# The om products of a gated attention and mLSTM layer dealt out between groups of the neighbouring projections

## The chip, the cores and the metric

The kernel runs on one core of a Trainium2 chip. The metric is the device time of one execution in microseconds (us), as the median of several runs of the same program. Lower is better. A profile is one further execution, taken with the hardware profiler on; its span runs from the first to the last recorded instruction.

## The reference, cut to what matters

One layer is computed for 256 tokens of width 1024, all in float32: an attention branch with 8 heads and an mLSTM branch with 4 heads, each multiplied with gates, summed, and projected back.

```python
h = _rmsnorm(x, norm_w) * (1 + scale) + shift
(qa, ka, va, za, qm, km, vm, zm, om, ig, fg, ga, gm) = jnp.split(h @ w_in, SPLIT_IDX, axis=-1)
...
ya = (ya * jax.nn.silu(za)) @ w_att_proj
...
hm = jax.nn.sigmoid(heads(om, ML_HEADS).astype(f32)) * hm
hm = _rmsnorm(hm, ml_norm_w.reshape(ML_HEADS, 1, ML_HEAD_DIM))
ym = (merge(hm).astype(x.dtype) * jax.nn.silu(zm)) @ w_ml_proj

y = jax.nn.sigmoid(ga) * ya + jax.nn.sigmoid(gm) * ym
return x + gate * (y @ w_out)
```

Nearly all the work is `h @ w_in` (1024 x 11272) and three more products with 1024 x 1024 weights. In the text, "om" is the projection whose sigmoid multiplies the mLSTM output, "vm" the mLSTM's values, "ga" and "gm" the two final gates, "ml" the projection `w_ml_proj`, and "att" the result of `w_att_proj`.

## The kernel before

**Groups.** After a first phase (normalisation, modulation, and the q and k projections of the attention) the weights go by in 98 groups. A group is two 128-row slices of a weight matrix, mostly 512 columns wide. Each float32 weight is split into a high part `wh` (ACT, a cast, L481) and a rest `wl` (DVE, a subtraction, L485; for eight groups POOL does it), and TensorE (PE) multiplies high by high, low by high and high by low. The function `split(g)` does the two steps for group g. The buffers for `wh` and `wl` hold five groups (`HB = 5`), and the main loop at step g first splits group g + 4, then evacuates the PSUM tile that has just been finished, then runs the step's hooks (small pieces of other work, listed by `at`), and then issues the matmuls of group g. So ACT and DVE work up to four groups ahead of PE, and the cast of split g + 4 cannot start before PE has finished group g - 1.

**Order of the groups before.** va 0 to 11, za 12 to 19, qm 20 to 27, km 28 to 35, att 36 to 43, zm 44 to 51, vm 52 to 59 (its first half 52 to 55, its second 56 to 59), om 60 to 73, ga 74 to 81, gm 82 to 89, ml 90 to 97, and the output projection. Each half of a segment has four groups and one PSUM tile (two such tiles, "mm").

**om by sums.** om is not multiplied in the plain way. Its weight is cut into 2 x 2 blocks of 512 x 512, and seven block products replace eight, in the manner of Strassen. Sums of rows of h (`h_full`, `h_sum`: P5, P6, P3, P7) are made on DVE and ACT while vm runs. Four sums of weight blocks are made in DRAM: eight DMAs from the POOL queue (`om_sum`, L746 and L748, four of them adding onto DRAM), issued at steps 10, 15, ... 45. The seven products collect in four PSUM banks ("aux", 128 x 512): bank 0 by products 0 and 2, bank 1 by 1 and 3, bank 2 by 4 and 6, bank 3 by 5. Between two products of one bank, `ev_om` takes the bank over: after product 0 ACT copies it with its sign turned (omu, L790), after product 1 DVE adds (omu, L792), after 3 DVE adds (omv, L796), after 4, 5 and 6 DVE subtracts (L798, L801, L804) and ACT takes the sigmoid (L785). A product is two groups of 6 matmuls; a vm group is 12 matmuls of the same size, a ga or gm group is 24 matmuls of half the width.

**After om.** Two groups at a time, `ml_num` (L872 to L879) multiplies the scores with vm, DVE multiplies with om's sigmoid and ACT takes the squares; `ml_y` (L887 to L898) normalises two heads over DVE, POOL and DVE; `ml_T` (L909 to L914) transposes the result on PE for the ml product, ACT and DVE splitting it (`ymh`, `yml`). `ev_ga` (L811, L812) evacuates ga's tile with a sigmoid on ACT into a buffer of its own (slot s5, which the scores occupied until then) and multiplies with att on POOL.

**Loads.** Weights come through six buffers ("raw", 1 MB each) by DMAs from SP's queue, in the order of the list `loads`. A buffer is refilled when its last split is done; `issue` keeps to the list's order.

Of the kernel before, what the change touches and what calls it, by code (L numbers as in the profile page):

```python
# [9 lines left out]
F32 = mybir.dt.float32  # L10
F32R = mybir.dt.float32r
AF = mybir.ActivationFunctionType
OP = mybir.AluOpType
# [38 lines left out]
OM_FIRST = (0, 1, 4, 5)  # L52
OM_SUMS = ((0, (0, 0), False), (2, (0, 1), False), (0, (0, 1), True), (2, (1, 1), True),
           (1, 0, False), (1, (1, 1), True), (3, 1, False), (3, (1, 0), True))
OM_SUM_AT = 10
W_PIECES = ((0, 512), (512, NR), (512, 1024), (1024, NR))


# [13 lines left out]
def tile_hybrid(ctx: ExitStack, tc: tile.TileContext, x, c, params2, w_row, w_va, ada_mod, ada_gate,  # L72
# [274 lines left out]
    seg("ws", wml, 0, "ml", "ym")  # L347
    seg("tok", wout, 0, "out", "y")
    NCH = len(chunks)
    C, G0, place = {}, [], []  # L350
    for i, ch in enumerate(chunks):
        C[ch["name"], ch["half"]] = i
        G0.append(len(place))
        place += [(i, kp) for kp in range(2 if ch["kind"] == "sums" else 4)]
    NG = len(place)
    G0.append(NG)

    def start(name, half=0):
        return G0[C[name, half]]

    def done(name, half):
        return G0[C[name, half] + 1]

    loads = []
    raw_of = {}
    last_use = {}

    def add_load(fn):
        loads.append(fn)
        return len(loads) - 1  # L370
# [6 lines left out]
    def mk_single(i, q):  # L377
        def f():
            v = raw_tile()[:, 0:4 * NV]
            nc.sync.dma_start(v, w_va[i, q])  # L380
            return v.rearrange("p (k n) -> p k n", k=4)
        return f

    def mk_pair(src, c0, kp):
        def f():
            t = raw_tile()
            v = t.rearrange("p (k n) -> p k n", k=2)
            nc.sync.dma_start(v, src[:, 2 * kp:2 * kp + 2, c0:c0 + 1024])
            return v
        return f  # L390

    om_sums = [dram.tile([128, 4, 512], F32, name=f"om_sum{i}") for i in range(4)]

    def om_block(kh, nh):
# [6 lines left out]
    def mk_block(blk):  # L401
        def f():
            v = raw_tile().rearrange("p (k n) -> p k n", k=4)
            nc.sync.dma_start(v, om_operand(blk))
            return v
        return f
# [1 line left out]
    NSINGLE = 3  # L408
    GSEG = ("km", "att", "zm", "vm")
    gate_loads = []  # L410
    for i, ch in enumerate(chunks):
        if i < NSINGLE:
            for q in range(2):
                li = add_load(mk_single(i, q))
                for g in (2 * q, 2 * q + 1):
                    raw_of[4 * i + g] = (li, slice(2 * (g % 2), 2 * (g % 2) + 2), slice(0, ch["n"]))
                last_use[li] = 4 * i + 2 * q + 1
        elif ch["kind"] == "sums":
            li = add_load(mk_block(ch["blk"]))
            for kp in range(2):  # L420
                raw_of[G0[i] + kp] = (li, slice(2 * kp, 2 * kp + 2), slice(0, 512))
            last_use[li] = G0[i] + 1
        elif ch["half"] == 0:
            if ch["name"] in GSEG:
                gate_loads.append(add_load(mk_pair(ada_gate, 0, len(gate_loads))))
            for kp in range(4):
                li = add_load(mk_pair(ch["src"], ch["c0"], kp))
                for hf in range(2):
                    raw_of[G0[i + hf] + kp] = (li, slice(0, 2), slice(hf * 512, hf * 512 + 512))
                last_use[li] = G0[i + 1] + kp  # L430
    xload = add_load(lambda: None)

    issued = [0]
# [26 lines left out]
    def slot(tag, shape, dt, name):  # L460
        free(tag)
        return hl.tile(shape, dt, name=name, tag=tag, bufs=1)
# [317 lines left out]
    def ev_om(j):  # L780
        om, b = T["om"], T["ombank"]
        part = [[om[:, t, 512 * n:512 * n + 512] for n in range(2)] for t in range(2)]

        def put(t, n, src):
            nc.scalar.activation(part[t][n], src, AF.Sigmoid)  # L785

        if j == 0:
            T["u"] = hl.tile([128, 2, 512], F32, name="omu", tag="scr", bufs=2)
            T["v"] = hl.tile([128, 2, 512], F32, name="omv", tag="scr", bufs=2)[:, 0]
            nc.scalar.mul(T["u"][:, 0], b[0], -1.0)  # L790
        elif j == 1:
            nc.vector.tensor_tensor(T["u"][:, 1], b[1], T["u"][:, 0], op=OP.add)  # L792
        elif j == 2:
            put(0, 0, b[0])
        elif j == 3:
            nc.vector.tensor_tensor(T["v"], b[1], T["u"][:, 0], op=OP.add)  # L796
        elif j == 4:
            nc.vector.tensor_tensor(part[1][1], T["v"], b[2], op=OP.subtract)  # L798
            put(1, 1, part[1][1])
        elif j == 5:  # L800
            nc.vector.tensor_tensor(part[1][0], b[3], T["v"], op=OP.subtract)  # L801
            put(1, 0, part[1][0])
        else:
            nc.vector.tensor_tensor(part[0][1], T["u"][:, 1], b[2], op=OP.subtract)  # L804
            put(0, 1, part[0][1])

    def ev_ga(pt, half):
        if half == 0:
            T["ga"] = slot("s5", [128, KT, S], F32, "gat")
        v = T["ga"][:, 4 * half:4 * half + 4]  # L810
        nc.scalar.activation(v, pt, AF.Sigmoid)  # L811
        nc.gpsimd.tensor_tensor(v, v, T["att"][:, 4 * half:4 * half + 4], op=OP.mult)  # L812

    def ev_gm(pt, half):
        if half == 0:
# [115 lines left out]

    def gate_read():
        gd = T["gd"]
        T["gateb"] = slot("s4", [128, D], F32, "gateb")
        nc.sync.dma_start(T["gateb"], bass.AP(tensor=gd.tensor, offset=gd.offset, ap=[[0, 128], [1, D]]))

    def load_x():
# [78 lines left out]
    for q, name in enumerate(("P5", "P6", "P3", "P7")):  # L1016
        at(s + 1 + q, h_sum, name)
    for hp in range(2):
        s = done("om", 6) + 3 * hp
        at(s + 1, ml_num, 2 * hp)  # L1020
        at(s + 2, ml_num, 2 * hp + 1)
        at(s + 3, ml_y, hp)
        at(s + 7, ml_T, 2 * hp)
        at(s + 8, ml_T, 2 * hp + 1)
# [24 lines left out]
    for g in range(NG):  # L1049
        ci, kp = place[g]  # L1050
        ch = chunks[ci]
        if g + A < NG:
            split(g + A, hooks_between.get(g, []))
            consumed.update(li for li in cons.get(g + A, []) if li not in gate_loads)
        if kp == 0:
            if ci > 0:
                pc = chunks[ci - 1]
                if pc["kind"] == "sums":
                    ev_om(pc["half"])
                elif pc["name"] in EV and ci - 1 != C["za", 0]:  # L1060
                    EV[pc["name"]](mmt[ci - 1], pc["half"])
                elif pc["name"] == "out":
                    for t in range(2):
                        ev_out(mmt[ci - 1][:, t], pc["half"] * 512, 512, t)
            sh = [128, 2, 512] if ch["kind"] == "tok" else [128, 4, 256]
            if ch["kind"] == "sums":
                if ch["half"] == 0:
                    T["ombank"] = []
                if ch["bank"] == len(T["ombank"]):
                    T["ombank"].append(aux([128, 512]))  # L1070
            elif ci < NCH - 1:
                mmt[ci] = ps.tile(sh, F32, name="mm", bufs=2)
                if ch["kind"] == "tok":
                    mmt[ci] = mmt[ci][:, :, 0:ch["n"]]
# [113 lines left out]
```

## Time and profile before

| | us |
|---|---|
| median of 3 runs | 355.19 (354.45 to 355.51) |
| the profiled execution's own time | 355.22 |
| its span | 353.4 |
| PE busy in the span | 344.1 |
| DVE busy | 268.3 |
| ACT busy | 220.5 |
| granted PE clock | 1.00 in every slice |

The span and the time of the profiled execution differ by 1.8 us. PE's busy time counts each matmul from its start to its end, and matmuls overlap: consecutive 512-wide ones start 0.23 us apart and are recorded with 0.39 us each. So PE's idle time is less than what PE loses; the losses are seen in the distance from start to start.

### The profile page before, as it was taken

The page shows a single profiled execution, that of the slowest core. Times are in us where ns is not written, and L with a number is a line of the kernel's source. Part 1 is how long each engine was busy: PE and PEld are TensorE (multiplying, and loading weights), DVE is VectorE, ACT ScalarE, POOL GpSimd, SP SyncE. Part 2 cuts the span into 40 slices and gives each one's busy share as a digit, 9 for nine tenths or more (in the row PEclk, how much of TensorE's full clock was granted, in tenths as well). Part 3 has the DMA queues.
Part 4 walks back from the last instruction along what each step waited for, and adds up shares of the span by engine and source line. Part 5 has one row for each costly group of instructions (what it writes and reads, how often), then busy time and mean ns, then how long its engine had stood idle before and what let it go on. Part 6 is the DMA issues. An engine that isn't in the chain of part 4 may idle for free.

```text
span 353.4 us, 6216 instructions
## 1 busy us (share of the span) xinstructions
PE 344.1 (97%) x2420; PEld 320.2 (91%) x2420; DVE 268.3 (76%) x390; ACT 220.5 (62%) x344; POOL 101.3 (29%) x89
## 2 busy tenths in 40 slices
PE   7999999999999999999999999998999999999996
PEld 7787889999999999999998888876799989999996
DVE  6989987966984348978847778789755667799961
ACT  4858789799777857657437654498454336932510
POOL 4600003942304473457005542000002212093000
PEclk9999999999999999999999999999999999999999
DMA  8999999883783899796996987569749007781011
GB/s 303 417 414 415 415 418 410 218 357 123 267 327 121 189 308 238 270 417 153 310 426 197 273 337 258 198 227 365 239 87 366 26 2 231 305 280 79 2 59 61
DMA packets 27309, 89.33 MB, mean 253 GB/s; under 512 B 3176, under 2 KB 5104, under 8 KB 26096
## 3 DMA queue, kind: packets, MB, share of 16 engines
q1 hardware_dynamic: 24408, 80.02, 61.2%
q0 software_dynamic: 2720, 8.39, 10.5%
q10 hardware_dynamic: 152, 0.53, 0.5%
q8 instruction: 19, 0.31, 0.3%
q14 instruction: 10, 0.08, 0.1%
HBM read 87.68 MB, written 9.64 MB: 275 GB/s over the span
## 4 chain that ended last, share of the span: by engine, by line
PE 69%; DVE 13%; issue 10%; ACT 5%; POOL 3%; ACTq 0%; POOLq 0%; DVEq 0%
PE pm L203 13%; PE mm L1120 8%; PE mm L1118 8%; PE mm L1121 8%; DVE wl L485 7%; PE mm L1113 5%; PE mm L1111 5%; PE mm L1112 5%; ACT wh L481 3%; PE mm L1104 1%; DVE kmT L715 1%; DVE omt L898 1%; PE xps L268 1%; PE aux L675 1%; PE mm L1133 1%
## 5 line engine op out<-in xcount | busy, mean ns | idle before, releaser
L485 DVE TENSOR_TENSOR wl<-raw,wh 128x1024 fp32r<-128x1024 f32 (+1 forms) x98 | 128.3, 1333 | 46.6 <-ACT wh L481 46.4
L481 ACT CAST wh<-raw 128x1024 fp32r<-128x1024 f32 (+1 forms) x106 | 105.1, 1016 | 27.6 <-DMA raw<-in_w_in_dram 11.3
L1118 PE MATMUL mm<-hTh,wh 128*128 128x256 f32 x320 | 90.1, 281 | 0.0
L1120 PE MATMUL mm<-hTl,wh 128*128 128x256 f32 x320 | 88.7, 277 | 0.0
L1121 PE MATMUL mm<-hTh,wl 128*128 128x256 f32 x320 | 88.7, 277 | 0.0
L1120 PEld LDWEIGHTS mm<-hTl,wh 128*128 128x128 f32 x320 | 60.2, 188 | 0.0
L1118 PEld LDWEIGHTS mm<-hTh,wh 128*128 128x128 f32 x320 | 60.2, 188 | 0.0
L1121 PEld LDWEIGHTS mm<-hTh,wl 128*128 128x128 f32 x320 | 60.2, 188 | 0.0
L1111 PE MATMUL mm<-wh,hTh 128*128 128x512 f32 (+1 forms) x112 | 40.6, 362 | 0.0
L1112 PE MATMUL mm<-wl,hTh 128*128 128x512 f32 (+1 forms) x112 | 40.2, 359 | 0.0
L1113 PE MATMUL mm<-wh,hTl 128*128 128x512 f32 (+1 forms) x112 | 40.2, 359 | 0.0
L485 POOL TENSOR_TENSOR wl<-raw,wh 128x1024 fp32r<-128x1024 f32 x8 | 20.5, 2573 | 16.7 <-ACT wh L481 16.7
L1113 PEld LDWEIGHTS mm<-wh,hTl 128*128 128x128 f32 x112 | 21.0, 188 | 2.5
L188 ACT CAST wrh<-raw 128x512 fp32r<-128x512 f32 (+1 forms) x24 | 18.2, 761 | 8.1 <-DMA raw<-in_w_row_dram 8.1
L1111 PEld LDWEIGHTS mm<-wh,hTh 128*128 128x128 f32 x112 | 21.1, 188 | 2.4
L1112 PEld LDWEIGHTS mm<-wl,hTh 128*128 128x128 f32 x112 | 21.1, 188 | 2.4
L193 DVE TENSOR_TENSOR wrl<-raw,wrh 128x512 fp32r<-128x512 f32 (+1 forms) x26 | 20.5, 813 | 1.4 <-ACT wrh L188 1.4
L203 PE MATMUL pm<-wrh,hTh 128*128 128x512 f32 x64 | 20.0, 393 | 0.0
L203 PE MATMUL pm<-wrh,hTl 128*128 128x512 f32 x64 | 19.9, 392 | 0.0
L203 PE MATMUL pm<-wrl,hTh 128*128 128x512 f32 x64 | 19.2, 398 | 0.0
L891 POOL TENSOR_SCALAR f<-f 128x4 f32<-128x4 f32 x2 | 0.4, 198 | 62.9 <-DVE f L890 62.9
L1121 PE MATMUL mm<-ymh,wl 128*128 128x256 f32 x64 | 17.7, 276 | 0.0
(245 smaller groups left out, 755.1 us busy)
## 6 DMA issues: line engine op xcount, KB each, us to landing
raw<-in_w_in_dram SPq DMA_DIRECT2D x31, 1024.0 KB, 7.4
adat<-in_ada_mod_dram SPq DMA_DIRECT2D x16, 512.0 KB, 8.8
om_sum<-in_w_in_dram POOLq DMA_DIRECT2D x6, 1024.0 KB, 10.0
raw<-in_w_va_dram SPq DMA_DIRECT2D x6, 688.0 KB, 8.9
raw<-in_ada_gate_dram SPq DMA_DIRECT2D x4, 1024.0 KB, 7.5
raw<-in_w_att_proj_dram SPq DMA_DIRECT2D x4, 1024.0 KB, 9.0
raw<-om_sum SPq DMA_DIRECT2D x4, 1024.0 KB, 5.1
raw<-in_w_ml_proj_dram SPq DMA_DIRECT2D x4, 1024.0 KB, 5.3
```

The lines of the kernel that those rows point to most:

```text
L188: copy(wsp[k][0][:, c0:c1], wrow[k][:, c0:c1])
L193: e.tensor_tensor(l[:, cs], wrow[k][:, cs], h[:, cs].bitcast(F32), op=OP.subtract)
L203: nc.tensor.matmul(pm[ch][:, t], a[:, k, t * 128:(t + 1) * 128], b[:, cs], start=k == 0 and i == 0, stop=k == KT - 1 and i == 2)
L268: nc.tensor.matmul(o, v, diag[:, t], start=t == 0 and kk == 0, stop=t == 1 and kk == 1, skip_group_check=True)
L481: nc.scalar.copy(h, w)
L485: e.tensor_tensor(l, w, h.bitcast(F32), op=OP.subtract)
L1111: nc.tensor.matmul(o, a, wh[:, kk], start=first, stop=False)
L1112: nc.tensor.matmul(o, a, wl[:, kk], start=False, stop=False)
L1113: nc.tensor.matmul(o, b, wh[:, kk], start=False, stop=last)
L1118: nc.tensor.matmul(o, wh[:, kk, cs], sh_[:, k], start=first and i % 2 == 0, stop=False, skip_group_check=True)
L1120: nc.tensor.matmul(o, wh[:, kk, cs], sl_[:, k], start=False, stop=False, skip_group_check=True)
L1121: nc.tensor.matmul(o, wl[:, kk, cs], sh_[:, k], start=False, stop=last and i % 2 == 1, skip_group_check=True)
```

## The change

The seven om products no longer stand together. `place`, which lists the groups in PE's order, now deals them out: after the first group of vm's second half, seven times one further group (vm's other three, then the four of ga's first half) and then the two groups of one om product. om begins at group 58, and ga's second half at 78; gm begins at 82 and ml at 90 as before. Three things follow in the same diff.

- Loads are listed in the order of first use. ga's weights come as four loads of four slices by 512 columns instead of four loads of two slices by 1024 columns, so that the first half can come without the second.
- `ev_ga` puts the sigmoid into a small buffer and multiplies att in place on POOL, so that it no longer needs slot s5; the row of the output gate (`gateb`) takes slot s5 instead of att's slot s4.
- The DMAs that sum om's blocks are issued at steps 6, 11, ... 41 instead of 10, 15, ... 45. `ev_om` now stands before the step's split, not behind it, and the second pair of heads' hooks (`ml_num`, `ml_y`, `ml_T`) follow the first pair's by 2 steps instead of 3.

```diff
-OM_SUM_AT = 10
+OM_SUM_AT = 6
...
+    for i, ch in enumerate(chunks):
+        if ch["kind"] == "sums" or ch["name"] == "ga" and ch["half"] == 0:
+            continue
+        if (ch["name"], ch["half"]) != ("vm", 1):
+            place += [(i, kp) for kp in range(4)]
+            continue
+        whole = [(ci, kp) for ci in (i, C["ga", 0]) for kp in range(4)]
+        place += whole[:1]
+        for j in range(7):
+            place += whole[1 + j:2 + j] + [(C["om", j], kp) for kp in range(2)]
...
+    def mk_quad(src, c0, q):
+        def f():
+            v = raw_tile().rearrange("p (k n) -> p k n", k=4)
+            nc.sync.dma_start(v, src[:, 4 * q:4 * q + 4, c0:c0 + 512])
+            return v
+        return f
...
     def ev_ga(pt, half):
-        if half == 0:
-            T["ga"] = slot("s5", [128, KT, S], F32, "gat")
-        v = T["ga"][:, 4 * half:4 * half + 4]
-        nc.scalar.activation(v, pt, AF.Sigmoid)
-        nc.gpsimd.tensor_tensor(v, v, T["att"][:, 4 * half:4 * half + 4], op=OP.mult)
+        T["ga"] = T["att"]
+        v = T["att"][:, 4 * half:4 * half + 4]
+        w = hl.tile([128, 4, S], F32, name="gat", tag="scr", bufs=2)
+        nc.scalar.activation(w, pt, AF.Sigmoid)
+        nc.gpsimd.tensor_tensor(v, v, w, op=OP.mult)
...
-        T["gateb"] = slot("s4", [128, D], F32, "gateb")
+        T["gateb"] = slot("s5", [128, D], F32, "gateb")
...
     for hp in range(2):
-        s = done("om", 6) + 3 * hp
+        s = done("om", 6) + 2 * hp
...
     for g in range(NG):
         ci, kp = place[g]
         ch = chunks[ci]
+        pi = ended.get(g)
+        if pi is not None and chunks[pi]["kind"] == "sums":
+            ev_om(chunks[pi]["half"])
         if g + A < NG:
             split(g + A, hooks_between.get(g, []))
...
+        if pi is not None:
+            pc = chunks[pi]
+            if pc["name"] in EV and pi != C["za", 0]:
+                EV[pc["name"]](mmt[pi], pc["half"])
```

Where the order stood out by hand before, it is shown by what is queued on the engines. DVE's queue before, from the splits of om's product 2 (products count from 0) to the addition that follows product 3 (omv); L485 is a split's subtraction, raw_2381, raw_2416, raw_2438, raw_2459 and raw_2506 are the loads of products 2 to 6, L740 belongs to vm's evacuation, and aux is the PSUM bank that an addition reads:

```order
L485 TENSOR_TENSOR wl_2555<-raw_2381,wh_2554 128x1024
L740 TENSOR_TENSOR vml_2478<-mm_2482,vaug_2477 128x2x512
L485 TENSOR_TENSOR wl_2568<-raw_2381,wh_2567 128x1024
L485 TENSOR_TENSOR wl_2580<-raw_2416,wh_2579 128x1024
L485 TENSOR_TENSOR wl_2594<-raw_2416,wh_2593 128x1024
L485 TENSOR_TENSOR wl_2606<-raw_2438,wh_2605 128x1024
L792 TENSOR_TENSOR omu_2583<-aux_2586,omu_2583 128x512
L485 TENSOR_TENSOR wl_2617<-raw_2438,wh_2616 128x1024
L485 TENSOR_TENSOR wl_2629<-raw_2459,wh_2628 128x1024
L485 TENSOR_TENSOR wl_2640<-raw_2459,wh_2639 128x1024
L485 TENSOR_TENSOR wl_2652<-raw_2506,wh_2651 128x1024
L796 TENSOR_TENSOR omv_2584<-aux_2586,omu_2583 128x512
```

DVE's queue at the same place in the changed kernel; L504 is the split's subtraction, raw_2381 is product 2, raw_2483 product 3, raw_2531 product 4, raw_2416 and raw_2533 are the two loads of ga's first half:

```order
L504 TENSOR_TENSOR wl_2547<-raw_2381,wh_2546 128x1024
L504 TENSOR_TENSOR wl_2563<-raw_2381,wh_2562 128x1024
L504 TENSOR_TENSOR wl_2576<-raw_2416,wh_2575 128x1024
L811 TENSOR_TENSOR omu_2543<-aux_2566,omu_2543 128x512
L504 TENSOR_TENSOR wl_2587<-raw_2483,wh_2586 128x1024
L504 TENSOR_TENSOR wl_2603<-raw_2483,wh_2602 128x1024
L759 TENSOR_TENSOR vml_2474<-mm_2478,vaug_2473 128x2x512
L504 TENSOR_TENSOR wl_2615<-raw_2416,wh_2614 128x1024
L504 TENSOR_TENSOR wl_2630<-raw_2531,wh_2629 128x1024
L504 TENSOR_TENSOR wl_2661<-raw_2531,wh_2660 128x1024
L504 TENSOR_TENSOR wl_2673<-raw_2533,wh_2672 128x1024
L815 TENSOR_TENSOR omv_2544<-aux_2566,omu_2543 128x512
```

The addition to omu stood behind both splits of product 3 and the first of product 4; now it stands ahead of both splits of product 3, and a ga split stands between the products.

POOL's queue before, from the last sums of om's blocks to the low parts of the mLSTM's q and k (qms, kms); om_sum1 and om_sum3 are blocks in DRAM, and the rows with DMA issue transfers:

```order
L746 DMA om_sum1_566<-in_w_in_dram 512x1x512
L485 TENSOR_TENSOR wl_1923<-raw_1562,wh_1922 128x1024
L748 DMA om_sum3_568<-om_sum1_566 16x16384
L843 TENSOR_TENSOR kms_2187<-kmT_1790,kms_2187 128x512
L843 TENSOR_TENSOR qms_2188<-qmT_1513,qms_2188 128x1024
L746 DMA om_sum3_568<-in_w_in_dram 512x1x512
```

POOL's queue at this place in the changed kernel:

```order
L765 DMA om_sum1_566<-in_w_in_dram 512x1x512
L504 TENSOR_TENSOR wl_1787<-raw_1562,wh_1786 128x1024
L504 TENSOR_TENSOR wl_1895<-raw_1729,wh_1894 128x1024
L504 TENSOR_TENSOR wl_1923<-raw_1562,wh_1922 128x1024
L767 DMA om_sum3_568<-om_sum1_566 16x16384
L765 DMA om_sum3_568<-in_w_in_dram 512x1x512
L862 TENSOR_TENSOR kms_2188<-kmT_1791,kms_2188 128x512
L862 TENSOR_TENSOR qms_2189<-qmT_1514,qms_2189 128x1024
```

The addition into om_sum1 moved ahead of two more splits on POOL, and the last addition, into om_sum3, moved ahead of kms and qms.

More of the change, by code (lines that the diff above doesn't have):

```diff
@@ L349, in tile_hybrid @@
     NCH = len(chunks)
-    C, G0, place = {}, [], []
+    C = {}
     for i, ch in enumerate(chunks):
         C[ch["name"], ch["half"]] = i
-        G0.append(len(place))
-        place += [(i, kp) for kp in range(2 if ch["kind"] == "sums" else 4)]
-    NG = len(place)
-    G0.append(NG)
+    place = []
+    for i, ch in enumerate(chunks):
[8 more added lines that the diff above has]
+            place += whole[1 + j:2 + j] + [(C["om", j], kp) for kp in range(2)]
+    NG = len(place)
+    G0, GE_ = {}, {}
+    for g, (ci, kp) in enumerate(place):
+        G0.setdefault(ci, g)
+        GE_[ci] = g + 1
+    ended = {g: ci for ci, g in GE_.items()}
     def start(name, half=0):
@@ L361, in done @@
     def done(name, half):
-        return G0[C[name, half] + 1]
+        return GE_[C[name, half]]
     loads = []
     raw_of = {}
+    quad, pair = {}, {}
     last_use = {}
@@ L410, in tile_hybrid @@
     gate_loads = []
[L411 to L430, printed above, removed]
+    for g, (i, kp) in enumerate(place):
+        ch = chunks[i]
+        if kp == 0 and ch["name"] in GSEG and ch["half"] == 0:
+            gate_loads.append(add_load(mk_pair(ada_gate, 0, len(gate_loads))))
+        if ch["kind"] == "sums":
+            if kp == 0:
+                add_load(mk_block(ch["blk"]))
+            raw_of[g] = (len(loads) - 1, slice(2 * kp, 2 * kp + 2), slice(0, 512))
+        elif i < NSINGLE or ch["name"] == "ga":
+            if kp % 2 == 0:
+                quad[i] = add_load(mk_single(i, kp // 2) if i < NSINGLE else mk_quad(ch["src"], ch["c0"] + 512 * ch["half"], kp // 2))
+            raw_of[g] = (quad[i], slice(2 * (kp % 2), 2 * (kp % 2) + 2), slice(0, ch["n"]))
+        else:
+            if ch["half"] == 0:
+                pair[ch["name"], kp] = add_load(mk_pair(ch["src"], ch["c0"], kp))
+            c0 = 512 * ch["half"]
+            raw_of[g] = (pair[ch["name"], kp], slice(0, 2), slice(c0, c0 + 512))
+        last_use[raw_of[g][0]] = g
     xload = add_load(lambda: None)
@@ L1054, in tile_hybrid @@
             consumed.update(li for li in cons.get(g + A, []) if li not in gate_loads)
-        if kp == 0:
[L1056 to L1064, printed above, removed]
+        if pi is not None:
+            pc = chunks[pi]
+            if pc["name"] in EV and pi != C["za", 0]:
+                EV[pc["name"]](mmt[pi], pc["half"])
+            elif pc["name"] == "out":
+                for t in range(2):
+                    ev_out(mmt[pi][:, t], pc["half"] * 512, 512, t)
+        if kp == 0:
             sh = [128, 2, 512] if ch["kind"] == "tok" else [128, 4, 256]
```

## The prediction

> **What bounds the kernel now.** I read the page first, then PE's waits, then the stretch around om instruction by instruction.
>
> ```profile
> PE 344.1 (97%) x2420; PEld 320.2 (91%) x2420; DVE 268.3 (76%) x390; ACT 220.5 (62%) x344; POOL 101.3 (29%) x89
> ```
>
> PE is the bound almost everywhere, so time can only come from PE's own losses. The list of PE's waits (who waited, for whom, us in total, times, longest) says where these are; L1094 is the first matmul of an om group, L909 the transposes of ml_T, L855 the scores:
>
> ```profile
> PE aux L1094 <- DVE omu L792: 1.6, 1, 1.6
> PE aux L909 <- DVE omt L898: 0.7, 2, 0.4
> PE aux L1094 <- DVE omt L798: 0.5, 1, 0.5
> PE aux L1094 <- ACT omu L790: 0.4, 1, 0.4
> PE aux L855 <- POOL qms L843: 0.3, 1, 0.3
> PE aux L909 <- ACT den L877: 0.3, 1, 0.3
> ```
>
> Three waits of 2.5 us together lie inside om, each for the engine that takes a bank over between two products. The others follow in ml_T, and one comes before, at the scores. What they cost is read from starts, since an interrupted stream also restarts slowly. PE's timeline at om's first matmuls, at the longest wait, at ga's first matmul behind om and at ml's first:
>
> ```profile
> 231.41 0.39 PE L1094 MATMUL aux<-wh,hTh 128*128 128x512 f32 x1
> 232.99 0.39 PE L1095 MATMUL aux<-wl,hTh 128*128 128x512 f32 x1
> 234.13 0.39 PE L1094 MATMUL aux<-wh,hsum 128*128 128x512 f32 x1
> ...
> 242.03 0.50 PE L1094 MATMUL aux<-wh,hsum 128*128 128x512 f32 x1 [1.59 <-DVE omu L792]
> ...
> 253.87 0.28 PE L1118 MATMUL mm<-hTh,wh 128*128 128x256 f32 x1
> ...
> 305.53 0.28 PE L1118 MATMUL mm<-ymh,wh 128*128 128x256 f32 x1
> 308.25 0.28 PE L1118 MATMUL mm<-ymh,wh 128*128 128x256 f32 x1
> ```
>
> The first 12 om matmuls take 234.13 - 231.41 = 2.72 us, so the 84 of all seven products would take 19.04 us. They take 253.87 - 231.41 = 22.46 us. **om loses 3.42 us.** Why, is seen on DVE and ACT in the same stretch:
>
> ```profile
> 231.40:242.00 10.60, 8.63 (x37) 6.50 (x35) 10.34 (x11) 10.31 (x12) 0.00 (x0) 1.00 0.83 285
> ...
> 231.26 0.69 DVE L769 TENSOR_TENSOR hsum<-omt,hsum 128x512 fp32r<-128x512 f32 x1 [0.69 <-ACT hsum L768]
> 232.21 3.50 DVE L485 TENSOR_TENSOR wl<-raw,wh 128x1024 fp32r<-128x1024 f32 x3 [0.26 <-ACT wh L481]
> 235.62 1.22 DVE L740 TENSOR_TENSOR vml<-mm,vaug 128x1024 fp32r<-128x1024 f32 x1
> 236.75 4.62 DVE L485 TENSOR_TENSOR wl<-raw,wh 128x1024 fp32r<-128x1024 f32 x4
> 241.29 0.68 DVE L792 TENSOR_TENSOR omu<-aux,omu 128x512 f32<-128x512 f32 x1
> ...
> 234.88 2.00 ACT L481 CAST wh<-raw 128x1024 fp32r<-128x1024 f32 x2
> 236.78 0.58 ACT L790 ACTIVATE omu<-aux 128x512 f32<-128x512 f32 x1
> ```
>
> The first row gives PE, weight loads, DVE and ACT in 10.6 us: DVE busy 10.34, ACT 10.31, with PE waiting. A split costs DVE 4.62 / 4 = 1.16 us and PE needs one per om group, 6 matmuls or 1.36 us; with a bank addition of 0.68 and vml of 1.22 on top, DVE falls behind. The addition L792 is queued behind four splits, and PE's next product waits for it.
>
> **The change part by part.**
>
> *The products dealt out.* PE's work is the same matmuls. Two om groups and one vm or ga group now take 1.36 x 2 + 2.72 = 5.44 us on PE (24 half-wide matmuls: 308.25 - 305.53 = 2.72), with three splits, 3.5 us, on DVE. The sums of h precede om as before, so DVE arrives at the same moment: group 62, the second of product 1, needs the split that ends at 232.21 + 3.50 / 3 = 233.4. PE reaches its L1095 at 232.99, because 58 and 59 now cost 1.36 each and 60 costs 2.72. **A new wait of 0.45 us.** From there I walk on with the durations quoted (cast 1.0, split 1.16, and the hooks). Bank 0 is taken over on ACT at step 60, ahead of that step's cast, and ends by 233.7, while product 2 starts at 237.3. The omu addition ends by 238.8, while product 3 starts at 242.7. For L798's successor, PE has groups 72 to 75, 8.2 us, between the end of product 4 and the start of product 6. So all three waits go: **-3.42 + 0.45.**
>
> *DVE through to the end of the mixed stretch.* From 231.95 it owes 20 splits (23.2), one vml (1.2), four bank operations (2.7) and three round trips over ACT's sigmoid:
>
> ```profile
> 257.12 2.36 DVE L485 TENSOR_TENSOR wl<-raw,wh 128x1024 fp32r<-128x1024 f32 x2 [1.63 <-ACT wh L481]
> ```
>
> that is 4.9 more, 32.0 in all, so it is done at 264. PE starts group 60 at 231.41 - 2.72 = 228.69 in both kernels and is through with om at 228.69 + 6 x 5.44 + 0.45 = 261.8. Three groups and three ml_num (1.1 each, below) lie before group 81, which needs the last of these splits at 273.2. DVE is 9 us ahead there.
>
> *ga's gate.* ACT waited for slot s5 until the fourth ml_num was done, and then POOL's multiplication ran against ml_y:
>
> ```profile
> 272.40 1.03 ACT L811 ACTIVATE gat<-mm 128x1024 f32<-128x1024 f32 x1 [2.60 <-PE aux L874]
> 273.51 2.53 POOL L812 TENSOR_TENSOR gat<-gat,attT 128x1024 f32<-128x1024 f32 x1 [1.02 <-ACT gat L811]
> 272.52 3.80 DVE L898 SCALAR_TENSOR_TENSOR omt<-omt,f,zmt 128x256 f32<-128x256 f32 x4 [1.73 <-POOL f L893]
> 287.02 1.67 DVE L898 SCALAR_TENSOR_TENSOR omt<-omt,f,zmt 128x256 f32<-128x256 f32 x4 [1.70 <-POOL f L893]
> ```
>
> The same four L898 took 3.80 us beside that multiplication and 1.67 without it. The 2.60 us wait goes with the slot. The first multiplication moves to step 76, the second to 82, both beside splits and bank or head work: price 0 to 3.80 - 1.67 = 2.1 us of DVE each. I take 2.1, as it is the same multiplication. The first is hidden by the 9 us just found, the second counts below.
>
> *After om.* Now 16 half-wide groups, four ml_num of 9 matmuls each and 16 transposes lie between 253.87 and 305.53:
>
> ```profile
> L1118 PE MATMUL mm<-hTh,wh 128*128 128x256 f32 x128 | 35.9, 280 | 0.0
> L874 PE MATMUL aux<-vaug,SD 128*128 128x258 f32 x12 | 3.4, 282 | 0.0
> L909 PE MATMUL aux<-ident,omt 128*128 128x128 f32 x16 | 2.7, 281 | 1.0 <-DVE omt L898 0.7 <-ACT den L877 0.3
> ```
>
> The 384, 36 and 16 matmuls at 0.113 us give 49.4; the stretch takes 51.66, so it loses 2.2. The 1.0 of it that is waiting, with some 0.1 to 0.2 at each of three restarts, is 1.5. It comes from DVE and ACT arriving late: ml_y's second set of L898 starts at 287.02, and ml_T stands four groups behind it on PE. DVE now enters the stretch on time and without the 2.60 and the 2.1. The second pair of heads comes a group sooner behind the first (2 steps, not 3). Walked on with the second multiplication's 2.1, the L898 that ml_T's third turn needs ends near 291.8, where PE arrives at 291.5; the other turns find theirs done. So 0.3 of the 1.5 stays and I take **-1.2**, with 0 and -2.2 as the ends.
>
> [...]
>
> *Loads.* Product 4, ga's second load and product 5 now wait for vm's last buffer and are issued together near 234.6. A landing takes, on the sums' lines and on loads in this stretch:
>
> ```profile
> DMA to landing us min/median/max: 4.7/5.1/13.8
> raw<-in_w_in_dram SPq DMA_DIRECT2D x6, 1024.0 KB, 5.0
> ```
>
> Three megabytes together I put at 8 us. The first is cast at 242.3 and its matmuls stand at 248.2, so some 11 us are free behind the issue: cost 0.
>
> *Sums begun sooner.* POOL is in no chain here but the scores', and each of its issues takes POOL 0.6 to 1.2 us by the rows below; where one comes to stand ahead of a split, that split's group is four steps away on PE. The transfers matter before the scores:
>
> ```profile
> 164.07 1.16 POOL L746 DMA_DIRECT2D om_sum<-in_w_in_dram  x1
> 175.85 0.56 POOL L748 DMA_DIRECT2D om_sum<-om_sum  x1 [8.18 <-DMA om_sum<-in_w_in_dram]
> 191.66 1.14 POOL L746 DMA_DIRECT2D om_sum<-in_w_in_dram  x1
> 184.55 2.00 ACT L481 CAST wh<-raw 128x1024 fp32r<-128x1024 f32 x2 [4.58 <-DMA raw<-in_w_in_dram]
> 167.70 4.93 SPq L388 DMA_DIRECT2D raw<-in_w_in_dram  x3
> ```
>
> The sum at 164.07 takes 11.8 us, until POOL's next issue may start. zm's last load, the third of SP's three, goes out at 172.3. ACT waits 4.58 us for it, the scores' parts behind it in ACT's queue come late, and PE waits the 0.3 for qms. The last two sums move to about 168 and 177. They may free that load (down to -0.6 with the restart) or press on it. I take 0.
>
> *Sum.* 355.22 - 3.42 + 0.45 - 1.2 = 351.05, forecast **351.1 us**; the profiled execution is 0.03 above the median.
>
> **The rivals.**
>
> *Late loads in the mixed stretch.* If the three loads take the longest 13.8 us, product 4 is there at 248.4, split 2.2 us later at 250.6, and PE, whose second matmul of that group stands at 248.4, waits 2.2. Against it: no sum runs then. 351.05 + 2.2 = 353.3.
>
> *The heads' chain stays late.* ml_y's second L898 set started at 287.02, while PE was at the first matmul of that step here:
>
> ```profile
> 274.88 0.28 PE L1118 MATMUL mm<-hTh,wh 128*128 128x256 f32 x1
> ```
>
> That is 12.1 us behind. If this lag stays, the fourfold gap of 4 x 2.72 + 0.9 = 11.8 us is too short, the waits in ml_T return and grow by half a microsecond: 355.22 - 3.42 + 0.45 + 0.5 = 352.8. For it: two steps instead of three. Against it: the lag's sources are gone.
>
> *Slower: the last sum stops zm's and vm's loads.* Moved from 191.66 to 177, it falls on the loads that ACT is already waiting for. Beside a sum a load lands in 9.4 us instead of 5.0:
>
> ```profile
> raw<-in_w_in_dram SPq DMA_DIRECT2D x2, 1024.0 KB, 9.4
> ```
>
> That is 4.4 us more; at worst the load is held for a sum's whole 11.8 us, and 351.05 + 11.8 gives 362.9. The kernel is slower from a delay of 5.3 us on (4.2 gained and 1.1 of measurement). Against it: zm's last load goes out 5 us before that sum. [...]
>
> *The tail takes it back.* POOL multiplies the last weights with gateb, in four pieces:
>
> ```profile
> 317.83 3.37 POOL L946 TENSOR_TENSOR raw<-raw,gateb 128x1024 f32<-128x1024 f32 x1
> ```
>
> They end at 321.2. The step whose split needs them begins 8 x 2.72 us after ml does, at 327.3 before and near 323.1 in the new time, so even if gateb did not come sooner, nothing is lost there. Should DVE and POOL still set the end by another way, nothing is gained: 355.2.
>
> **How the numbers follow.** Forecast 0.60, late loads 0.14, late chain 0.13, slower 0.06, no change 0.07 (the doubled load time among it). The forecast's own range is 349.4 (all 2.2 behind om and the 0.6 at the scores) to 352.3 (none of the 1.2). Taking in the two middle rivals, 349.4 to 353.4 holds over 0.8. A measurement of this kernel tells about 0.3%, 1.1 us, from no change; both middle rivals lie beyond it. So faster 0.87, same 0.07, slower 0.06.
>
> **What would show it.** Right: no waits of om's matmuls for omu or omt, one short wait for wl at the second product, gat without a wait for PE, the distance from om's first group to ml's first shorter by 4 us, and ml_T's waits at most 0.3. Wrong: casts waiting for raw between 234 and 250, ml_T waiting for L898's successor by over 1 us, or the scores' matmuls waiting longer for qms than 0.34. The forecast falls if PE's waits in om only change their names.

## The result, and the profile after

| | before | after |
|---|---|---|
| median of 6 runs each, us | 354.76 (354.22 to 355.51) | 352.86 (352.05 to 353.93) |
| ratio | 1 | 0.9946, 95% interval 0.9925 to 0.9967 |
| profiled execution, us (span) | 355.22 (353.4) | 352.05 (350.2) |

The kernel is faster, by 1.9 us or 0.5% at the medians. The forecast was 4.1. The profiled execution of the changed kernel is the fastest of its six, and gains 3.2 against that of before. The page after:

```profile
PE 343.5 (98%) x2420; PEld 321.3 (92%) x2420; DVE 266.0 (76%) x390; ACT 220.2 (63%) x344; POOL 100.2 (29%) x89
```

PE's waits after, all of them (who waited for whom, us in total, times, longest; L1115 is an om matmul, L1124 one of the output projection, L848 the cast of ml's result; the one for ident is at the start and as before):

```profile
PE mm L1124 <- ACT yh L848: 1.6, 1, 1.6
PE warm L232 <- POOL ident masks.py:199: 1.4, 1, 1.4
PE aux L1115 <- DVE wl L504: 0.3, 1, 0.3
```

All the waits that the prediction quoted are gone from the list, those in om, in ml_T and at the scores. The short one for `wl` stands where it was forecast. But a wait of 1.6 us has come up in the output projection. To see what each stage gained, I cut PE's timeline at four starts. Before (att's first matmul, zm's first, ml's last):

```profile
160.75 0.28 PE L1118 MATMUL mm<-yah,wh 128*128 128x256 f32 x1
...
182.51 0.40 PE L1111 MATMUL mm<-wh,hTh 128*128 128x512 f32 x1
...
350.02 0.28 PE L1133 MATMUL mm<-wh,yl 128*128 128x256 f32 x1
```

After (att's first, zm's first, om's first, the wait for wl, ga's second half, ml's first, the last one):

```profile
160.43 0.36 PE L1138 MATMUL mm<-yah,wh 128*128 128x256 f32 x1
...
182.28 0.40 PE L1131 MATMUL mm<-wh,hTh 128*128 128x512 f32 x1
...
225.13 0.39 PE L1114 MATMUL aux<-wh,hTh 128*128 128x512 f32 x1
...
231.93 0.39 PE L1114 MATMUL aux<-wh,hsum 128*128 128x512 f32 x1
232.65 0.50 PE L1115 MATMUL aux<-wl,hsum 128*128 128x512 f32 x1 [0.33 <-DVE wl L504]
...
261.65 0.28 PE L1138 MATMUL mm<-hTh,wh 128*128 128x256 f32 x1
...
301.12 0.28 PE L1138 MATMUL mm<-ymh,wh 128*128 128x256 f32 x1
...
346.76 0.28 PE L1153 MATMUL mm<-wh,yl 128*128 128x256 f32 x1
```

With ml's first matmul before at 305.53 (quoted in the prediction), the distances are: stage A, the eight groups behind att, 21.76 before and 21.85 after; stage B, zm's first to ml's first matmul, 123.02 and 118.84, **4.18 us less**; stage C, ml's first to the last matmul, 44.49 and 45.64, **1.15 us more**. So the middle of the kernel gave as much as was forecast for the whole, and the end took a quarter of it back. Of the 4.18, however, 0.61 stands ahead of om: from zm's first to om's first matmul it was 48.90 before, and it is 42.85 and two groups of 2.72 now. That is the wait for qms, which e5 will show to be chance.

Why om no longer waits shows on DVE. Here are 10 us around the first bank take-overs, in the columns PE, weight loads, DVE, ACT; the stretch that the prediction shows was 10.6 us long:

```profile
231.90:241.90 10.00, 9.67 (x53) 8.10 (x52) 9.98 (x10) 9.71 (x12) 0.00 (x0) 1.00 0.82 307
...
237.16 0.68 DVE L811 TENSOR_TENSOR omu<-aux,omu 128x512 f32<-128x512 f32 x1
```

DVE is as full as before, but the addition L811 now ends at 237.8, 4.3 us before PE wants its bank, for product 3 at 242.2. Before, it ended at 242.0 with PE standing.

The new wait at the end, from four engines' timelines: POOL's four multiplications by gateb, DVE's splits and evictions of ml, ACT's cast, and the matmul that waits.

```profile
303.96 5.82 POOL L965 TENSOR_TENSOR raw<-raw,gateb 128x1024 f32<-128x1024 f32 x2 [13.23 <-DMA gateb<-gd]
316.00 5.20 POOL L965 TENSOR_TENSOR raw<-raw,gateb 128x1024 f32<-128x1024 f32 x2 [6.22 <-DVE yf L846]
...
306.04 9.36 DVE L504 TENSOR_TENSOR wl<-raw,wh 128x1024 fp32r<-128x1024 f32 x6 [0.46 <-ACT wh L500]
315.33 0.68 DVE L846 TENSOR_TENSOR yf<-mm,gmt 128x512 f32<-128x512 f32 x1
316.04 2.90 DVE L847 TENSOR_TENSOR yf<-yf,attT 128x512 f32<-128x512 f32 x1
318.86 0.68 DVE L846 TENSOR_TENSOR yf<-mm,gmt 128x512 f32<-128x512 f32 x1
319.57 2.17 DVE L847 TENSOR_TENSOR yf<-yf,attT 128x512 f32<-128x512 f32 x1
...
323.38 4.63 DVE L504 TENSOR_TENSOR wl<-raw,wh 128x1024 fp32r<-128x1024 f32 x4 [0.26 <-ACT wh L500]
327.93 0.68 DVE L846 TENSOR_TENSOR yf<-mm,gmt 128x512 f32<-128x512 f32 x1
328.64 0.69 DVE L847 TENSOR_TENSOR yf<-yf,attT 128x512 f32<-128x512 f32 x1
...
329.37 0.62 ACT L848 CAST yh<-yf 128x512 fp32r<-128x512 f32 x1 [3.17 <-DVE yf L847]
...
330.04 0.39 PE L1124 MATMUL mm<-wh,yh 128*128 128x256 f32 x1 [1.55 <-ACT yh L848]
```

Look at the two additions L847. Free, one takes 0.69 us (the row at 328.64). Beside POOL's third and fourth product they take 2.90 and 2.17. That is 3.7 us of DVE, and everything queued behind on DVE is later by it: four splits, then the second evictions, then the cast for which PE waits. Before, POOL's four products, DVE's splits and the first eviction stood so:

```profile
308.78 12.42 POOL L946 TENSOR_TENSOR raw<-raw,gateb 128x1024 f32<-128x1024 f32 x4 [13.58 <-DMA gateb<-gd]
...
309.42 12.87 DVE L485 TENSOR_TENSOR wl<-raw,wh 128x1024 fp32r<-128x1024 f32 x4 [0.54 <-ACT wh L481]
322.21 0.68 DVE L827 TENSOR_TENSOR yf<-mm,gmt 128x512 f32<-128x512 f32 x1
```

The products ran beside splits that PE did not need yet, and the evictions began when POOL had finished. That was not free either: the second evictions started 3.84 us behind the end of ml's matmuls (331.13 and 327.29). Now they start 5.05 us behind it (327.93 and 322.88); without the products (e2) it is 2.36.

### The profile page after: what moved, and what is told of

Same layout as the page of the kernel before. It is cut to its first block, busy times and chain, and to the rows that moved or that the text cites. A ratio compares the mean times of both kernels' runs of the same rounds, so it can differ in the third digit from the quotient of the medians.

```text
span 350.2 us, 6218 instructions
## 1 busy us (share of the span) xinstructions
PE 343.5 (98%) x2420; PEld 321.3 (92%) x2420; DVE 266.0 (76%) x390; ACT 220.2 (63%) x344; POOL 100.2 (29%) x89
## 4 chain that ended last, share of the span: by engine, by line
PE 83%; DVE 9%; ACT 4%; issue 3%; POOL 1%; ACTq 0%; POOLq 0%; DVEq 0%
PE pm L203 13%; PE mm L1138 13%; PE mm L1140 13%; PE mm L1141 12%; PE mm L1131 5%; PE mm L1132 5%; PE mm L1133 5%; DVE wl L504 3%; ACT wh L500 2%; DVE yf L847 2%; PE aux L1115 2%; PE aux L1116 1%; PE mm L1124 1%; PE aux L1114 1%; PE xps L268 1%
## 5 line engine op out<-in xcount | busy, mean ns | idle before, releaser
L504 DVE TENSOR_TENSOR wl<-raw,wh 128x1024 fp32r<-128x1024 f32 (+1 forms) x98 | 123.2, 1281 | 46.1 <-ACT wh L500 46.0
L504 POOL TENSOR_TENSOR wl<-raw,wh 128x1024 fp32r<-128x1024 f32 x8 | 20.4, 2566 | 17.8 <-ACT wh L500 17.8
L831 POOL TENSOR_TENSOR attT<-attT,gat 128x1024 f32<-128x1024 f32 x2 | 5.3, 2626 | 50.1 <-ACT gat L830 50.1
L1138 PE MATMUL mm<-yah,wh 128*128 128x256 f32 x64 | 17.7, 277 | 0.0
```

The source lines that it names most:

```text
L504: e.tensor_tensor(l, w, h.bitcast(F32), op=OP.subtract)
L1138: nc.tensor.matmul(o, wh[:, kk, cs], sh_[:, k], start=first and i % 2 == 0, stop=False, skip_group_check=True)
```

## The experiments

Theory A says that the missing gain went into that tail, by the products falling on ml's evictions. Rival B lays it on the order of DVE's queue or on late loads of out's weights, whatever POOL does. C holds ml's eight groups, which take 21.76 us in some executions and 22.6 in others, in both orders (see e1 and e5). All times stand beside the kernel before, run on the same chip. The table gives the ratio with its 95% interval and the stages of one trace of each (differences of PE's starts, as above).

| kernel | median us | ratio | A | B | C |
|---|---|---|---|---|---|
| before | 354.76 | 1 | 21.76 | 123.02 | 44.49 |
| e5 before again | 355.04 | 1.0006 (0.9993 to 1.0019) | 21.76 | 122.42 | 44.65 |
| e6 before, no products | 354.84 | 0.9982 (0.9968 to 0.9997) | 21.76 | 123.08 | 44.33 |
| e7 before, ga in place | 354.99 | 0.9993 (0.9983 to 1.0003) | 21.75 | 123.36 | 44.33 |
| after | 352.86 | 0.9946 (0.9925 to 0.9967) | 21.85 | 118.84 | 45.64 |
| e1 after again | 353.18 | 0.9948 (0.9922 to 0.9974) | 22.69 | 119.12 | 45.46 |
| e2 after, no products | 352.09 | 0.9911 (0.9886 to 0.9936) | 22.69 | 119.13 | 44.33 |
| e3 after, gateb earlier | 352.04 | 0.9917 (0.9891 to 0.9943) | 22.69 | 119.13 | 44.56 |
| e4 after, gate at the end | 352.55 | 0.9915 (0.9884 to 0.9947) | 22.69 | 119.13 | 44.32 |
| e8 after, sums at 10 | 352.19 | 0.9919 (0.9901 to 0.9937) | 21.76 | 118.85 | 45.72 |
| e9 after, one sum later | 352.06 | 0.9917 (0.9904 to 0.9930) | 21.76 | 119.10 | 45.61 |
| e10 after, om part dealt | 353.29 | 0.9948 (0.9936 to 0.9960) | 21.85 | 121.42 | 43.57 |
| e11 sums at 10, gateb earlier | 351.83 | 0.9927 (0.9899 to 0.9954) | 21.76 | 119.00 | 44.84 |
| e12 and h's sums sooner | 351.00 | 0.9894 (0.9881 to 0.9907) | 21.76 | 118.49 | 44.68 |

**e1, the changed kernel again.**

> The changed kernel itself, once more, beside the three variants of it that follow. Both theories: about 0.995 of the kernel before, 352.1 to 353.9 us, and TensorE again waits 1.2 to 1.8 us at the third group of out's first half for ScalarE's cast of ml's second half. If that wait is 0.5 or less here while the time is the same, the tail is not where the missing gain went.

Ratio 0.9948, as in the first measurement. But the tail's wait is 0.45 us here. By the sign in the expectation this speaks against the tail, so the sign has to be answered: ml's own eight groups took 22.62 us instead of 21.76, so PE came to the tail later and waited less, and C is 45.46 all the same. e8 and e9, with the quicker and the slower groups, have 45.72 and 45.61. DVE sets C in the changed kernel, and the wait's length is no measure of the loss. And stage A took 22.69 instead of 21.85. That was a second loss, not foreseen by either theory (e5, e8 and e9).

**e2, without the products.**

```diff
-    for q in range(4):
-        at(start("ml") + 3 + q, gate_columns, q)
```

> The changed kernel without GpSimd's four multiplications of the last weights by gateb; the second half of the output columns is then not gated. Theory A (products three and four run beside the first evictions of ml and hold VectorE there): the two additions of yf take 0.7 us each instead of 2.9 and 2.2, the tail's wait falls from 1.55 us to at most 0.4, and the kernel is 1.1 to 1.6 us faster than the repeat, near 351.5. Theory B (the order of VectorE's queue, four splits ahead of the second evictions, or the late loads of out's weights): the wait stays over 1 us and the time within 0.4 us of the repeat.

The wait is gone, C falls to 44.33, 1.1 us under the repeat, and the median by 1.1 us too (the intervals overlap). ml's groups ran at the slower pace in both traces. The same additions as above:

```profile
316.80 0.69 DVE L847 TENSOR_TENSOR yf<-yf,attT 128x512 f32<-128x512 f32 x1
...
318.13 0.69 DVE L847 TENSOR_TENSOR yf<-yf,attT 128x512 f32<-128x512 f32 x1
```

The order of DVE's queue is the same, so it is not the cause. out's last two loads do go out sooner, 7.0 us behind ml's first matmul instead of 9.5. But in the changed kernel DVE stands idle for no load between 306.04 and the second evictions (the rows above), so the loads set only when the products run. Rival B is out.

**e3, gateb read three steps sooner.**

```diff
-    at(start("gm") + 4, gate_read)
+    at(start("gm") + 1, gate_read)
```

> The changed kernel with gateb read three steps sooner; the computation is whole. Theory A: the first two products start when their weights land, near 300 instead of 304 us, end before the splits at 306, so buffers come free some 2 us sooner and the last two products start near 313 and end by 318.5; one eviction is stretched instead of two, the tail's wait falls under 0.5 us, 1.0 to 1.5 us faster than the repeat. Theory B: no change within 0.4 us. A third way: the first products now stretch the small VectorE operations of ml_T, and TensorE waits at ml's groups; then the time is the repeat's or worse, with that wait in the list.

1.1 us faster than the repeat at the medians (the intervals overlap), C less by 0.9. The way there differs from what was written. The first two products did run earlier (299.6 and 303.3), but the last loads did not land sooner: the last two products start at 317.06, not 313:

```profile
317.06 5.44 POOL L965 TENSOR_TENSOR raw<-raw,gateb 128x1024 f32<-128x1024 f32 x2 [11.35 <-DMA raw<-in_w_out_dram]
...
317.35 0.68 DVE L846 TENSOR_TENSOR yf<-mm,gmt 128x512 f32<-128x512 f32 x1
318.07 2.17 DVE L847 TENSOR_TENSOR yf<-yf,attT 128x512 f32<-128x512 f32 x1
320.16 3.50 DVE L850 TENSOR_TENSOR yl<-yf,yh 128x512 fp32r<-128x512 f32 x2
```

One addition (0.69 free) and the pair L850 (1.46 free) are stretched, by 3.5 us together. In e1 it was one addition of 2.79 and the pair at 3.50, 4.1 us together, and the first eviction began 13.9 us behind ml's first matmul, here 13.6. The two differences make up the 0.9.

L846, which reads PSUM and one SBUF tile, takes its usual 0.68 beside the running product; L847, which reads two SBUF tiles, takes 2.17 instead of 0.69.

**e4, the gate on DVE at the end.**

```diff
-        if c0 < 512:
-            nc.vector.tensor_tensor(o, pt, T["gateb"][:, cs], op=OP.mult)
-            pt = o
+        nc.vector.tensor_tensor(o, pt, T["gateb"][:, cs], op=OP.mult)
+        pt = o
```

The four products go as in e2.

> The changed kernel without GpSimd's four products; instead VectorE multiplies the second half of the output by gateb when it evicts it, as it does for the first half. The computation is whole. Theory A: the gain of the run without products, 1.1 to 1.6 us, less one multiplication of 128x256 on the path at the very end, some 0.4 us (half of the 0.69 us that the 128x512 one takes): 0.7 to 1.2 us faster than the repeat. Theory B: 0.3 to 0.5 us slower than the repeat.

0.6 us faster than the repeat by the medians and 1.2 by the ratios, with runs from 350.41 to 353.77, so the time alone tells little. C is as in e2, and the extra multiplication of 0.42 us stands behind the last matmul. The trace fits theory A.

**e5, the kernel before again; e6, without the products in the old order.** e6 drops the same two lines as e2.

> The kernel before, once more, for a second trace of it. The traces of the changed kernel show TensorE at two paces in unbroken stretches of matmuls of 256 columns: 0.1133 or 0.1177 us from one to the next, in the eight groups behind att and in the eight of ml 21.8 or 22.6 us. Theory P (the pace belongs to the execution, not to the change): this kernel too shows 22.6 us in those stretches in some executions, and its profiled time then is 0.9 us longer for each. Theory Q (only the changed kernel falls into the slow pace there): 21.8 us in both again. Ratio to the kernel before 0.997 to 1.003 in both.

> The kernel before without GpSimd's four multiplications of the last weights; the second half of the output columns is then not gated. In it the four products run beside four splits of VectorE, which take 12.87 us for 4.6 of work. Theory A (the products cost the kernel before little, the changed one more): the tail's wait of 0.35 us goes, 0.3 to 0.6 us faster than the kernel before; the three waits of om stay. Theory B (without products both kernels win the same, so the tail has no part in the missing gain): 1.0 us faster or more.

e5: 21.76 us behind att again. ml's eight groups took 21.76 here, but 22.61 in e6 and 22.62 in e7, which have the old order too. So the slow pace belongs to the execution in ml (P), and behind att only the changed kernel has shown it (Q). e5 has no wait for qms either, and 48.29 us from zm's first to om's first matmul; that wait of before's first trace, and 0.6 of the 4.18 with it, was chance.

e6 gains 0.6 us by the ratio (0.03 to 0.32%, or 0.1 to 1.1 us), where e2 gained 1.3 by the ratios. This interval reaches theory B's 1.0 too, so the time does not decide. The traces do at one pace. With ml's groups at the slower pace, C in the old order is 44.33 with the products (e7, which differs from before in ga's gate alone) and 44.33 without them (e6); in the new order it is 45.46 with them (e1) and 44.33 without (e2). There the products cost the old order nothing and the new one 1.1 us: theory A. At the quicker pace no trace lacks the products. C is 44.49 and 44.65 in the old order, 45.64 and 45.72 in the new (after, e8), again about 1.1 apart. But e10, which does not wait in the tail, has 43.57 at that pace, so the old order loses about 0.9 there too. e6's runs fall into two sets, four from 353.33 to 353.59 us and eight from 354.79 to 355.37; only one of the eight was traced, and whether the four had the quicker pace is open.

**e7, ga's gate alone in the old order.** `ev_ga` and the slot of gateb as in the change, all else as before.

> The kernel before with ga's gate alone changed: sigmoid into a scratch tile, att multiplied in place, gateb in slot s5. om is in its old order. Theory G (the gate's wait for slot s5 and the multiplication beside ml_y make ml_T late): the 2.60 us wait of ScalarE goes, the waits in ml_T fall from 1.0 to at most 0.3 us, 0.7 to 1.5 us faster than the kernel before. Theory O (ml_T is late because om left VectorE late): the waits in ml_T stay over 0.6 us, at most 0.4 us faster.

No gain (0.9993). ACT's 2.60 us wait is gone, and the waits in ml_T are not:

```profile
269.17 1.03 ACT L811 ACTIVATE gat<-mm 128x1024 f32<-128x1024 f32 x1
...
272.00 3.77 DVE L898 SCALAR_TENSOR_TENSOR omt<-omt,f,zmt 128x256 f32<-128x256 f32 x4 [1.74 <-POOL f L893]
...
PE aux L909 <- DVE omt L898: 0.7, 2, 0.4
...
PE aux L909 <- ACT den L877: 0.3, 1, 0.3
```

The wait for the slot is not what makes ml_T late, which leaves theory O. But L898 is stretched here too (3.77), so this run does not rule out the multiplication beside it as the cause; e10 does.

**e8, the sums in DRAM begun at step 10 again.**

```diff
-OM_SUM_AT = 6
+OM_SUM_AT = 10
```

> The changed kernel with the sums in DRAM begun at step 10 again, as before. Theory S (the earlier sums freed zm's loads): the scores wait 0.3 us for qms again, 0.4 to 0.8 us slower than the changed kernel (352.9 to 353.2 in its two measurements). Theory N (the 0.6 us that the changed kernel is ahead at group 56 come by chance of the pace): no wait for qms, no change within 0.3 us.

Neither. There is no wait for qms, but the ratio is 0.9919, 0.3% under the changed kernel's two (the intervals overlap), with A at 21.76. The trace carries more than the time here: beginning the sums sooner seems to have cost something. The traces say how. e1, POOL's queue, DVE's queue and att's first matmul (om_sum is the sixth sum; L944 is a step of the output gate's row sum, L734 the reading of km's PSUM tile, whose bank att's product takes over):

```profile
152.61 1.17 POOL L765 DMA_DIRECT2D om_sum<-in_w_in_dram  x1
153.34 2.88 POOL L504 TENSOR_TENSOR wl<-raw,wh 128x1024 fp32r<-128x1024 f32 x1
...
154.44 2.86 DVE L944 CUSTOM_DVE_ANT_0 raw<-raw,cbg,prm 128x1024 f32<-128x1024 f32 x1
...
158.38 2.42 DVE L734 SCALAR_TENSOR_TENSOR kmT<-mm,prm,kmT 128x255 f32<-128x255 f32 x6
...
160.94 0.35 PE L1138 MATMUL mm<-yah,wh 128*128 128x256 f32 x1
```

The sum's issue stands between two splits on POOL and pushes the second onto L944, which takes 2.86 us instead of 1.66. L734 then ends at 160.80, where att's first matmul was due at 160.84, 0.113 behind the one before it. PE hesitates by 0.1 us, too short for the list of waits, and from there the 192 matmuls come 0.1177 us apart instead of 0.1133: 0.9 us.

**e9, that one sum issued one step later.**

```diff
-        at(OM_SUM_AT + 5 * q, om_sum, i, src, add)
+        at(OM_SUM_AT + 5 * q + (q == 5), om_sum, i, src, add)
```

> The changed kernel with one of the eight sums in DRAM, the sixth, one step later, so that GpSimd issues it behind the split that it stood ahead of; nothing else moves. Theory H (GpSimd's issue pushes that split onto VectorE's gate sum, VectorE hands the bank to att's first matmul late, and the hitch of 0.06 to 0.1 us there sets TensorE to the slow pace): no hitch, the eight groups behind att take 21.8 us instead of 22.7, 0.6 to 1.0 us faster than the changed kernel: ratio to the kernel before 0.992. Theory T (the traffic of the earlier sums slows the stretch): 22.7 us again, ratio 0.995.

0.9917, and no hitch. The same places as in e1:

```profile
150.87 4.76 POOL L504 TENSOR_TENSOR wl<-raw,wh 128x1024 fp32r<-128x1024 f32 x2 [5.17 <-ACT wh L500]
155.57 1.14 POOL L765 DMA_DIRECT2D om_sum<-in_w_in_dram  x1
...
155.05 1.66 DVE L944 CUSTOM_DVE_ANT_0 raw<-raw,cbg,prm 128x1024 f32<-128x1024 f32 x1
...
157.77 2.42 DVE L734 SCALAR_TENSOR_TENSOR kmT<-mm,prm,kmT 128x255 f32<-128x255 f32 x6
...
161.45 0.28 PE L1138 MATMUL mm<-yah,wh 128*128 128x256 f32 x1
```

Only POOL's order moved, with seven of eight sums still early, so POOL's issue makes the hitch, and not the traffic (T). All 8 traces without the hitch have A at 21.75 or 21.76. Of 6 with it, 4 have 22.69, and 2, after and e10, 21.85. The four slow ones ran on one chip, on which no kernel without the hitch was traced; e10, with all sums early on the chip of e9, has the hitch and 21.85. So that the hitch brings the slow pace is not shown; whether the chip or chance decides there is open.

**e10, three of seven products dealt out.** vm's second half alternates with products 0 to 2; 3 to 6 follow in a row, then ga's first half.

```diff
-        whole = [(ci, kp) for ci in (i, C["ga", 0]) for kp in range(4)]
+        whole = [(ci, kp) for ci in (i,) for kp in range(4)]
```

(The condition that skips ga's first half in `place` goes, too.)

> The changed kernel with only the first three products of om dealt out among vm's second chunk; products 4 to 7 follow in a row and ga's first chunk stands behind them. Theory D (VectorE's debt is what made om wait, and three dealt products let it catch up): om's matmuls wait 0.8 us or less in all, the distance from the groups behind att to ml's first matmul is 119.3 to 120.3 us (119.1 with all dealt, 122.8 with none): 0.2 to 1.2 us slower than the changed kernel. Theory R (products in a row wait for each take-over whatever VectorE owes): 1.5 us or more of waits, distance over 121 us, 2 us slower.

The waits in om lie between the theories, the distance B of 121.42 in theory R's range, and the time is the changed kernel's, which neither forecast. In om 0.9 us of waiting is back besides the 0.3 for wl, and ml_T waits 1.4:

```profile
PE aux L928 <- DVE omt L917: 1.4, 2, 1.0
...
PE aux L1114 <- DVE omt L817: 0.9, 1, 0.9
...
257.12 0.68 DVE L823 TENSOR_TENSOR omt<-omu,aux 128x512 f32<-128x512 f32 x1
```

om's last subtraction L823 starts 5.55 us behind PE's end of om (251.57) here, and 3.62 in the changed kernel (265.27 and 261.65). That debt is carried to ml_T. Here ga's gate is the changed kernel's, and all eight multiplications L917 (L898 before) take their free 0.48 us each, so neither the slot nor a stretched multiplication is needed to make ml_T late. B is 2.6 us longer, and C, at 43.57, 2.1 shorter than after: the evictions come later, POOL's products again fall on splits, and the tail does not wait. What the middle loses the tail gives back.

**e11 and e12, the mends together.** e11 has the edits of e3 and e8; e12 also begins the sums of h one step sooner:

```diff
-    s = start("vm") + 1
+    s = start("vm")
     at(s, h_full)
```

> The changed kernel with the sums begun at step 10 as before and gateb read three steps sooner: the two mends together. If the losses are two and independent: no slow pace behind att and a tail of 44.5 instead of 45.6 us, 1.5 to 2.0 us faster than the changed kernel, ratio to the kernel before 0.989. If the pace only moves from one stretch to the next: ratio 0.992 as each alone.

> The same with the sums of h one step sooner, for the 0.33 us that the second om group waits for its split. Theory of the order (VectorE's operations for h ahead of it make that split late): no wait there and 0.3 to 0.5 us faster than the run before it. Rival (the operations for h now delay VectorE at the scores, whose parts wait in turn): a new wait at the scores or at zm's groups, no change or slower.

e11's interval (0.9899 to 0.9954) holds 0.992 and just misses 0.989, so by the time the two mends do not add up in full. In its trace the pace did not move on: A is 21.76, and so are ml's eight groups. But C is 44.84 where 44.5 was expected, with a tail wait of 0.8 left, so the second mend works in part only. e12 is 0.8 us under e11 by the medians (the intervals overlap). It has no wait for wl, and B is 0.35 to 0.6 us shorter than in the other kernels with all products dealt out. It is the fastest of the kernels here: 351.00 us, ratio 0.9894 (0.9881 to 0.9907), below the changed kernel's 0.9946, and the intervals do not meet.

## Why the prediction was right and wrong

- **om, -3.42 + 0.45: the mechanism right, the sum too large.** Its three waits are gone. The new one is at the place and of the size named: 232.65 - 231.93 = 0.72 us from start to start where 0.23 is usual, 0.49 lost. PE is through with om at 261.65, forecast 261.8, but that is luck. PE came to om's first matmul at 225.13, where the prediction's own 228.69 less a product's 2.72 gives 225.97, mostly because the wait for qms did not come. From there om with the two vm and four ga groups among it took 36.52 us; before, by 22.46 and six groups of 2.72, it was 38.78. The gain is 2.26, not 2.97. Dealing out had been put at nothing but the new wait. Yet each of ga's four groups takes 2.83 us behind an om product (matmuls 0.118 apart), not 2.72, and the om product behind it 2.75, not 2.72.
- **After om, -1.2 with 0.3 left: the sum right, a reason wrong.** 39.47 us where 51.66 less four ga groups made 40.78: 1.31 gained. PE's list has no wait in ml_T, but at its third turn, the one named, PE's weight load waits 0.33 us for L917. By e7 and e10, though, the gate's 2.60 and the stretched L898 were not needed for the waits; what these runs and the old order share is that om leaves DVE late. The price of 2.1 us for the second multiplication was not paid: it ran from 284.54 to 287.06, while DVE waited for a cast.
- **Loads, 0: right.** No cast waits for a load between 234 and 250. No run shows the doubled load time that the chance of no change takes in. Before, the load issued at 195.09 beside the last sum landed in 13.8 us and the next, issued at 209.89 behind it, in 5.1; the 9.4 given for a load beside a sum is the mean of these two. In the changed kernel the loads issued at 171.83 and 178.71, with the last sum under way (issued at 173.98, 17.6 us), landed in 11.2 and 13.2 us; ACT waited 4.43 us for the first of them, where it had waited 4.58, and PE did not wait for qms.
- **POOL's multiplication beside DVE: measured, and priced at the wrong place.** The prediction read it from L898 (3.80 us beside POOL's multiplication, 1.67 without it) and priced it at ga's gate, where the 2.1 us did not come. It did not ask the same of the tail, where L847 went from 0.69 us to 2.90 and 2.17 beside POOL's products, while L846, which reads PSUM, kept its 0.68.
- **"So even if gateb did not come sooner, nothing is lost there": the step that failed.** It compared the end of the products with the step whose split needs them, and asked only whether the products come in time. It did not ask on which DVE operations they fall. With ml 4.4 us earlier and out's last two loads not earlier at all (issued from 310.9 on, before from 308.9 on), the last two products moved from the splits ahead of the evictions onto the evictions. C is +0.98 (means of two traces each: 45.55 and 44.57). The old order was not free of it: it lost about 0.9 at the quicker pace of ml's groups (e6).
- **Sums sooner, "I take 0": the second.** "Where one comes to stand ahead of a split, that split's group is four steps away on PE" is true, but POOL's split also held up a DVE instruction (L944, 2.86 us in e1 instead of the 1.66 in e9), and that one's chain had no time to spare. Cost: 0.09 in one trace of the change, 0.93 in the other, where the slow pace came with it; that the hitch is what brings that pace is not shown.
- **Together.** The 0.7 that om gave too little and the 0.6 that the wait for qms gave by chance nearly cancel in the first pair of traces. B: 118.98 - 122.72 = -3.74 (means of two traces each, before and e5, after and e1). C: +0.98. A: +0.51. The sum is -2.25; the medians gave -1.90 and -1.97. The rival "the tail takes it back" named the right place, with POOL's products, at too large a price.

## What to carry to other kernels

When a stage becomes shorter, list what ran beside the following stage on engines that hold each other up (here GpSimd and VectorE, 0.69 us becoming 2.90), and slide it against the new times: asking whether it still ends in time isn't enough. A gain upstream is worth what the first engine without slack downstream lets through, so compare starts stage by stage, not waits alone. A step called free because its own result is needed late can still delay what stands beside it.

## What the runs showed of the hardware that was not expected

- Two paces of TensorE at a granted clock of 0.999 to 1.000: the 192 matmuls of 256 columns behind att, and the 192 of ml, came 0.1133 or 0.1177 us apart, at one pace to the end (eight groups: 21.76 or 22.6 us). Behind att the slow pace was seen only after a hitch of 0.06 to 0.1 us, and on one chip only. In ml both were seen for both orders. What sets it is open.
- Three VectorE additions of two SBUF tiles, started beside a running GpSimd multiplication, ended 0.55 us after it (2.17 to 2.90 us instead of 0.69, in the changed kernel and e1); the operation that reads PSUM and SBUF kept its 0.68 beside it (in the changed kernel and e3).
